# An instruction order from a timeline model: the scheduler of a hybrid-backbone kernel is given another machine model

## The chip, the cores and the metric

The kernel runs on one core of one Trainium2 chip. The metric is the device time of one execution in microseconds (us), the median of several runs. TensorE does the matmuls (PE; its weight loads are listed as PEld), VectorE is DVE, ScalarE is ACT, GpSimd is POOL, and SyncE (SP) issues most of the DMAs.

## The reference

One trunk layer over 256 latent and 256 context tokens of width 2048. One input projection feeds three mixers, which run in both directions over the tokens; each is projected, gated and merged, and a mixture of experts (MoE) follows.

```
u_lat = _modulate(_rmsnorm(x, g_norm1[i]), mod_lat[0], mod_lat[1])
cl = jnp.split(u_lat @ w_in, points, axis=-1)
ya_ctx, ya_lat = _bidirectional(_s5_direction, ...)      # A: S5, complex diagonal state
yb_ctx, yb_lat = _bidirectional(_rwkv_direction, ...)    # B: RWKV-7, matrix state, token by token
yc_ctx, yc_lat = _bidirectional(_gla_direction, ...)     # C: gated linear attention, chunks of 64
pa = _s5_out(ya, cols[0], s5_d, s5_w_glu)
pb = _rwkv_out(yb, cols[2], rw_g_up, rw_ln_w, rw_ln_b, rw_w_proj)
pc = _gla_out(yc, cols[7], gl_norm_g, gl_w_proj)
y = (gate_a * pa + gate_b * pb + gate_c * pc) @ w_out
x = x + mod_lat[2] * y_lat
v_lat = _modulate(_rmsnorm(x, g_norm2[i]), mod_lat[3], mod_lat[4])
x = x + mod_lat[5] * _moe(v_lat, ...)                    # top-1 group of 4, top-2 of its 8 experts
```

All operands are float32.

## The kernel before

**Dense work.** The large projections are done by `dense`. Each weight chunk is loaded by SP into `ww` (L348), rounded by ACT to `hw` (L350), and its remainder `lw` is formed by DVE, or at times by POOL (L355); the activations stand likewise as a rounded and a remainder tile (UH and UL; XA, XB, XC further on). Three matmuls, L386, L387 and L388, then add up hw·high, hw·low and lw·high; they are called dense matmuls below. A chunk is 12 of them. Buffers hold four `ww`, three `hw`, three `lw` and two accumulators `pd`.

**Stages, in time.** (1) The modulation vectors (weights `wm`, matmuls L256) and the input norm (L295, L297), while DVE prepares the S5 matrices (W of L1442 to L1448, used by the matmuls L1463). (2) S5 in two rounds, each for half of the states: the input matmuls L1552 fill a tile X; a scan of 63 steps on DVE (L1570 to L1573, four operations a step, each on the result of the one before) runs over X; then for four k and two directions DVE and POOL build an output matrix W (DVE L1594, L1596, L1598, L1599; POOL writes `wx` between), and matmuls L1615 and L1622 use it. There is one W buffer for each direction. (3) GLA. (4) RWKV-7 (L740 to L800): a chain of small matmuls and DVE steps from chunk to chunk; the second part of the modulation (L958, 64 loads of 1 MB into a single buffer `wm`) runs beside it. Its result `yo` leaves to DRAM by a DMA that POOL issues (L802). (5) `rw_out` loads it back as `yb` (L1173, on SP), takes each head's mean and variance (L1185 to L1197 on DVE, L1189 on ACT), transposes it (L62), multiplies it by the gate (L1206) and writes the operand XB. (6) Three branch projections: glu from XA, gl_proj from XC, rw_proj from XB; then w_out (L1226), the router (L1811) and the MoE, which streams 192 loads of 1 MB.

**What sets the order.** The source is written as Python generators that are merged in given proportions, so that dense work stands between the steps of the S5, GLA and RWKV chains. For instance,

```
merge((K.s5(), 320), (chainv(dense, n[0]), n[0]))
merge((chain(K.gla(sp), K.gla_out(sp)), 135), (chainv(dense, n[2]), n[2]))
K.rwkv(dense, steps, K.mods())
```

The order in which the source emits instructions is their priority. The framework's scheduler then goes through a model of the machine, takes for each engine a ready instruction of the best priority, and writes that order into the program. [...] Dense jobs of the S5 stage write through buffers of a pool that is closed when the stage ends, and those of the GLA stage through another, so dense work of a later stage cannot be taken in an earlier one.

## Time and profile before

| | us |
|---|---|
| median of 3 runs | 2418.14 (2417.78 to 2425.74) |
| the profiled execution | 2429.91 |
| its span in the trace | 2428.0 |
| PE busy | 2202.4 |
| DVE busy | 1451.3 |
| ACT busy | 922.8 |
| POOL busy | 440.3 |
| mean granted TensorE clock | 0.95 of full speed |

A busy time is the union of an engine's work. The span is 1.9 us shorter than the execution that it was taken from, which is itself 11.8 us above the median. In the page's slices PE is busy at eight to nine tenths or more until about 1800 us; after about 2000 us the DMA engines are full instead.

### The profile page before, as it was taken

To read this page: it belongs to the slowest core of one execution; us is meant where nothing else is said; L and a number is where in the kernel's file an instruction comes from. 1 tells how busy PE (TensorE), PEld (TensorE's weight loads), DVE (VectorE), ACT (ScalarE), POOL (GpSimd) and SP (SyncE) were. 2 spreads that over 40 slices of the span, in tenths; PEclk is the share of its full clock that TensorE was granted. 3 is DMA by queue.
4 is the path that set the end of the run, shared out by engine and by line. 5 is a ranking of instruction groups with operands and counts; after the bars stand their busy time and mean duration, and the time that the engine had idled before them with its cause. 6 is when DMAs were issued, how large, how long until landed. Compare 5 with 4: busy or idle time off the path is not lost. (4 is left out here: it accounts for less than half of the span.)

```text
span 2428.0 us, 49729 instructions
## 1 busy us (share of the span) xinstructions
PE 2202.4 (91%) x19317; PEld 1582.0 (65%) x19317; DVE 1451.3 (60%) x3816; ACT 922.8 (38%) x1833; POOL 440.3 (18%) x705
## 2 busy tenths in 40 slices
PE   7899989989989999999999999999998988887775
PEld 2447668767676777777888888988996753332211
DVE  8954967967666665656687877786764432211112
ACT  2235225236543434344445454543543431111111
POOL 2422033031212222222232222320021000000000
PEclk9999999989999999999999999999999989998876
DMA  7763332433276667667333232455667799999997
GB/s 287 289 213 105 126 112 85 131 121 107 88 254 212 229 216 246 227 208 236 101 116 99 94 115 90 127 161 163 201 200 261 241 380 422 421 421 421 421 422 297
DMA packets 188723, 526.05 MB, mean 217 GB/s; under 512 B 21376, under 2 KB 46992, under 8 KB 163520
## 3 DMA queue, kind: packets, MB, share of 16 engines
q1 hardware_dynamic: 172464, 500.14, 57.6%
q10 hardware_dynamic: 14160, 16.36, 1.9%
q0 software_dynamic: 1856, 6.29, 0.7%
q8 instruction: 154, 2.52, 0.4%
q14 instruction: 89, 0.73, 0.1%
HBM read 502.16 MB, written 19.51 MB: 215 GB/s over the span
## 5 line engine op out<-in xcount | busy, mean ns | idle before, releaser
L350 ACT CAST hw<-ww 128x512 fp32r<-128x512 f32 x556 | 340.2, 617 | 618.1 <-PE pd L387 505.3
L386 PE MATMUL pd<-UH,hw 128*128 128x256 f32 (+2 forms) x1648 | 566.0, 343 | 8.8 <-ACT hw L350 4.4
L388 PE MATMUL pd<-UH,lw 128*128 128x256 f32 (+2 forms) x1648 | 543.3, 330 | 10.1 <-DVE lw L355 7.0
L387 PE MATMUL pd<-UL,hw 128*128 128x256 f32 (+2 forms) x1648 | 538.8, 327 | 0.0
L355 DVE TENSOR_TENSOR lw<-ww,hw 128x512 fp32r<-128x512 f32 x544 | 389.6, 719 | 221.3 <-ACT hw L350 209.4
L386 PEld LDWEIGHTS pd<-UH,hw 128*128 128x128 f32 (+1 forms) x1648 | 314.3, 191 | 62.0 <-issue 14.1
L388 PEld LDWEIGHTS pd<-UH,lw 128*128 128x128 f32 (+1 forms) x1648 | 314.7, 191 | 57.7 <-DVE lw L355 13.6
L387 PEld LDWEIGHTS pd<-UL,hw 128*128 128x128 f32 (+1 forms) x1648 | 315.4, 191 | 37.0 <-issue 14.6
L1876 ACT ACTIVATE xg<-pm,modT,a 128x128 f32<-128x128 f32 x128 | 46.1, 484 | 307.2 <-PE pe L1900 283.9
L1900 PE MATMUL pe<-mw,xg 128*32 128x512 f32 x1024 | 139.1, 661 | 25.8 <-DMA mw<-in_moe_gu_dram 25.8
L1900 PEld LDWEIGHTS pe<-mw,xg 128*32 128x32 f32 x1024 | 27.7, 113 | 110.9 <-DMA mw<-in_moe_gu_dram 64.9
L1980 POOL TENSOR_TENSOR acc<-acc,mw 128x512 f32<-128x512 f32 x2 | 3.4, 1718 | 480.9 <-ACT acc L1979 480.9
L958 PE MATMUL pmod<-wm,sil 128*32 128x512 f32 x512 | 68.2, 605 | 21.6 <-DMA wm<-in_w_mod_dram 21.3
L1921 PE MATMUL pdn<-mw,ht 128*32 128x512 f32 x512 | 81.3, 697 | 3.5 <-ACT ht L1914 3.3
L1929 PE MATMUL pm<-ysl,owt 128*128 128x512 f32 x128 | 65.2, 633 | 20.4 <-DVE ysl L1926 20.4
L1873 PEld LDWEIGHTS pm<-oh,m 128*128 128x128 f32 x512 | 61.5, 197 | 25.5 <-issue 25.5
L388 PE MATMUL pd<-XAh,lw 128*128 128x256 f32 x256 | 73.3, 286 | 3.5 <-DVE lw L355 3.5
L256 PE MATMUL pmod<-wm,silu 128*32 128x512 f32 x256 | 62.3, 645 | 15.4 <-DMA wm<-in_w_mod_dram 14.7
L1909 DVE TENSOR_TENSOR hd<-hd,pe 128x256 f32<-128x256 f32 x8 | 3.4, 422 | 121.5 <-ACT hd L1908 121.5
L355 DVE TENSOR_TENSOR lx<-wx,hx 128x512 fp32r<-128x512 f32 x64 | 43.3, 691 | 53.8 <-ACT hx L350 52.9
L743 DVE TENSOR_TENSOR vz<-psa,z 32x256 f32<-32x256 f32 x120 | 50.1, 418 | 41.0 <-PE psa L740 39.2
L386 PE MATMUL pd<-XAh,hw 128*128 128x256 f32 x256 | 74.0, 289 | 0.0
(578 smaller groups left out, 4346.5 us busy)
## 6 DMA issues: line engine op xcount, KB each, us to landing
mw<-in_moe_gu_dram SPq DMA_DIRECT2D x128, 1024.0 KB, 19.8
wm<-in_w_mod_dram SPq DMA_DIRECT2D x64, 1024.0 KB, 5.4
mw<-in_moe_d_dram SPq DMA_DIRECT2D x64, 1024.0 KB, 19.7
ww<-in_w_gate_dram SPq DMA_DIRECT2D x192, 256.0 KB, 3.0
ww<-in_w_cols_dram SPq DMA_DIRECT2D x132, 256.0 KB, 2.9
wm<-in_w_mod_dram SPq DMA_DIRECT2D x64, 512.0 KB, 6.1
ww<-in_w_rkv_dram SPq DMA_DIRECT2D x96, 256.0 KB, 2.9
ww<-in_glu_dram SPq DMA_DIRECT2D x64, 256.0 KB, 2.9
```

Of the source, the lines that this page charges most:

```text
L256: nc.tensor.matmul(pt[32 * j:32 * j + 32, :], self.silu[:, k, :], w[:, k2, :], start=k < 4, stop=k >= 12, tile_position=(0, 32 * j))
L350: nc.scalar.copy(h, w)
L355: eng.tensor_tensor(l, w, h.bitcast(FT), op=OP.subtract)
L386: nc.tensor.matmul(ov, h[:, k2, :], uh, start=k == 0, stop=False)
L387: nc.tensor.matmul(ov, h[:, k2, :], ul, start=False, stop=False)
L388: nc.tensor.matmul(ov, l[:, k2, :], uh, start=False, stop=k == nk - 1)
L743: nc.vector.tensor_tensor(vz[bq, e, tt::2, :].rearrange(V, h=2), psa[bq, :, 0:128].rearrange("p h (d v) -> p h d v", d=2), z[bq, tt::2, :] ...
L958: nc.tensor.matmul(pt[32 * j:32 * j + 32], self.sil[:, 2 * kq + j, win], w[:, j], start=u == 0 and kq == 0, stop=u == 15 and kq == 6, tile ...
L1873: nc.tensor.matmul(p[:, 128 * (k % 4):128 * (k % 4) + 128], self.x2[:, t, 128 * k:128 * k + 128], oh[:, t, :], start=t == 0, stop=t == 1)
L1900: nc.tensor.matmul(pe[32 * e:32 * e + 32, :], xg[:, k, 32 * e:32 * e + 32], w[:, e, :], start=k == 0, stop=k == 15, tile_position=(0, 32 * e))
L1921: nc.tensor.matmul(py[32 * e:32 * e + 32, :], ht[:, f, 32 * e:32 * e + 32], w[:, e, :], start=f == 0, stop=f == 1, tile_position=(0, 32 * e))
L1929: nc.tensor.matmul(pr, owt[:, 128 * t:128 * t + 128], ys, start=True, stop=True)
```

## The change

A class of the name `tile` takes the place of the imported module. Its only function hands on the context with one more argument, so that the scheduler orders the instructions by its timeline model.

```
-import concourse.tile as tile
+import concourse.tile as _tile
...
+class tile:
+
+
+    @staticmethod
+    def TileContext(nc):
+        return _tile.TileContext(nc, schedule_with_timeline_sim=True)
+
```

Everything below moves down by 8 lines, so L386 is L394 in the changed kernel, and L1615 is L1623. The computing instructions, their engines, tiles and buffers are the same ones; their order on each engine is another. The rows below are the instruction lists of an engine, before and after; xN is a run of N alike, and the numbers behind the names tell tiles of one name apart.

**PE, the second round of S5**, at the last input matmuls (first piece) and at the first output matmuls (second piece) before the change. Between them stand 302 dense matmuls, and no other work.

```order
L388 MATMUL pd_4009<-UH_134,lw_4058 128x256
L386 MATMUL pd_4009<-UH_134,hw_4056 128x256
L1552 MATMUL pm_4153<-ug_1582,tr_4134 64x64 x14
L387 MATMUL pd_4009<-UL_135,hw_4056 128x256
L388 MATMUL pd_4009<-UH_134,lw_4058 128x256
```

```order
L1615 MATMUL py_5032<-W_5033,X_1581 32x128 x8
L1615 MATMUL py_5032<-W_5051,X_1581 32x128 x8
L386 MATMUL pd_5047<-UH_134,hw_4970 128x512
L387 MATMUL pd_5047<-UL_135,hw_4970 128x512
L388 MATMUL pd_5047<-UH_134,lw_4972 128x512
L1615 MATMUL py_5032<-W_5033,X_1581 32x128 x8
L1615 MATMUL py_5032<-W_5051,X_1581 32x128 x8
L386 MATMUL pd_5047<-UH_134,hw_5000 128x512
```

The same place after:

```order
L396 MATMUL pd_5635<-UH_134,lw_5664 128x256
L1560 MATMUL pm_4153<-ug_1582,tr_4134 64x64 x16
L1623 MATMUL py_5032<-W_5033,X_1581 32x128 x8
L1623 MATMUL py_5032<-W_5051,X_1581 32x128 x8
L1623 MATMUL py_5032<-W_5033,X_1581 32x128 x8
L1623 MATMUL py_5032<-W_5051,X_1581 32x128 x8
L1630 MATMUL py_5032<-T_5062,ug_1582 32x128 x8
L1623 MATMUL py_5032<-W_5129,X_1581 32x128 x8
L1623 MATMUL py_5032<-W_5140,X_1581 32x128 x8
```

The dense matmuls have moved ahead of the input matmuls; none is left between the last input matmul and the last output matmul of the round.

**DVE, the end of the same scan**, before and then after; L1573 (L1581 after) ends a step, and L355 forms an `lw`.

```order
L1573 TENSOR_TENSOR X<-X,s5t_5008 128x2x32
L355 TENSOR_TENSOR lw<-ww,hw 128x512
L1570 TENSOR_TENSOR s5t_5019<-LRI,X 128x64
L1571 TENSOR_TENSOR s5t_5020<-LRI,X 128x64
L1572 TENSOR_TENSOR X<-X,s5t_5019 128x64
L1573 TENSOR_TENSOR X<-X,s5t_5020 128x64
L355 TENSOR_TENSOR lw<-ww,hw 128x512 x2
L1594 TENSOR_TENSOR W<-s5KP,s5c 128x576
```

```order
L1581 TENSOR_TENSOR X<-X,s5t_5008 128x2x32
L1578 TENSOR_TENSOR s5t_5019<-LRI,X 128x64
L1579 TENSOR_TENSOR s5t_5020<-LRI,X 128x64
L1580 TENSOR_TENSOR X<-X,s5t_5019 128x64
L1581 TENSOR_TENSOR X<-X,s5t_5020 128x64
L1602 TENSOR_TENSOR W<-s5KP,s5c 128x576
L1604 TENSOR_TENSOR W<-s5KP,s5c 128x576
L1606 TENSOR_TENSOR W<-W,wx 128x576
```

The 26 L355 that stood within this scan are gone from it, and none stands among the builds of W that follow.

**PE, from the end of RWKV to `rw_out`**, before and then after. L798 (L806) is the last matmul of the chain, `yb` is the result loaded back.

```order
L388 MATMUL pd_21196<-XAh_19794,lw_21182 128x256
L798 MATMUL pj_20989<-z_20680,anti_5398 128x128 x2
L62 MATMUL pm_21003<-ident_82,modT_132 16x128
L386 MATMUL pd_21196<-XAh_19794,hw_21180 128x256
L387 MATMUL pd_21196<-XAl_19795,hw_21180 128x256
```

```order
L795 MATMUL py2_20922<-vz_20185,lmr_19984 32x64
L806 MATMUL pj_20989<-z_20680,anti_5398 128x128 x2
L70 MATMUL pm_21003<-ident_82,modT_132 16x128
L70 MATMUL pm_22081<-ident_82,yb_21017 128x128
L1214 MATMUL pm_22086<-glo_21022,gup_21020 128x256
L70 MATMUL pm_22152<-ident_82,yb_21017 128x128
```

Before, 513 rows of the glu projection (XA) stand between L62 on modT and the first L62 on yb; after, they stand earlier, between the steps of the RWKV chain, and the two L70 follow each other. In the RWKV stage the median number of dense matmuls between two L740 (L748) is 24 before and 39 after.

## Rows read from the trace of the kernel before

**Rows 1.** The page: busy us, share of the span and instructions of each engine.
```profile
PE 2202.4 (91%) x19317; PEld 1582.0 (65%) x19317; DVE 1451.3 (60%) x3816; ACT 922.8 (38%) x1833; POOL 440.3 (18%) x705
```

**Rows 2.** Windows: start:end, length, busy us of each engine (instructions), PEclk, DMA, GB/s.
```profile
407.00:516.00 109.00, 100.24 (x728) 78.37 (x723) 90.23 (x312) 27.51 (x51) 21.19 (x15) 0.95 0.37 113
...
700.00:1670.00 970.00, 941.88 (x10786) 767.03 (x10785) 685.57 (x1994) 450.35 (x880) 244.98 (x518) 0.99 0.51 166
1670.00:1780.00 110.00, 106.47 (x952) 105.52 (x951) 80.58 (x156) 58.58 (x109) 0.69 (x1) 0.98 0.63 196
1780.00:1965.00 185.00, 159.82 (x843) 133.28 (x841) 95.16 (x199) 71.94 (x140) 23.25 (x28) 0.91 0.75 257
1965.00:2428.00 463.00, 355.76 (x2224) 133.34 (x2224) 86.61 (x163) 65.61 (x177) 3.40 (x2) 0.85 0.97 402
```

**Rows 3.** Timeline of DVE, scan of round two: start, us, engine, line; one undisturbed step.
```profile
431.17 0.23 DVE L1570 TENSOR_TENSOR s5t<-LRI,X 128x64 f32<-128x64 f32 x1
...
431.96 0.23 DVE L1570 TENSOR_TENSOR s5t<-LRI,X 128x64 f32<-128x64 f32 x1
```

**Rows 4.** Windows over that scan and over the outputs behind it.
```profile
420.00:476.00 56.00, 53.34 (x248) 42.49 (x247) 52.39 (x249) 16.45 (x31) 0.00 (x0) 1.00 0.44 135
476.00:514.00 38.00, 32.43 (x408) 24.52 (x407) 26.34 (x29) 4.61 (x8) 16.53 (x11) 0.87 0.32 94
```

**Rows 5.** Timeline of DVE, six builds of W behind that scan: first and last row.
```profile
479.11 0.75 DVE L1594 TENSOR_TENSOR W<-s5KP,s5c 128x576 f32<-128x576 f32 x1
...
507.71 0.74 DVE L1599 SCALAR_TENSOR_TENSOR W<-W,wx 128x576 f32<-128x576 f32 x1
```

**Rows 6.** Groups of one line from 476 to 514 us: count, busy, mean ns, idle before.
```profile
L1615 PE MATMUL py<-W,X 64*32 64x128 f32 x256 | 10.5, 314 | 5.6 <-DVE W L1598 5.6
L1622 PE MATMUL py<-T,ug 128*32 128x128 f32 x64 | 2.6, 279 | 0.0
```

**Rows 7.** Windows around the router: PE before and behind a pause.
```profile
1960.00:1970.00 10.00, 6.02 (x27) 5.92 (x28) 5.65 (x38) 0.20 (x1) 0.00 (x0) 0.50 1.01 424
1970.00:1980.00 10.00, 10.00 (x87) 4.60 (x85) 0.00 (x0) 3.01 (x8) 0.00 (x0) 0.97 0.72 279
```

**Rows 8.** Timeline row, then line views, in `rw_out`: count, ns min/median/max, first and last start.
```profile
1675.28 0.69 POOL L802 DMA_DIRECT2D dyb<-yo  x1 [6.14 <-DVE yo L800]
...
DMA to landing us min/median/max: 2.5/2.6/4.0
...
L1173 SPq DMA_DIRECT2D yb<-dyb x2: 327/370/412, 1678.1 to 1678.9; - x2
...
DMA to landing us min/median/max: 5.6/6.0/6.5
...
L1185 DVE TENSOR_REDUCE rws<-yb x4: 676/678/686, 1683.7 to 1688.4; 128x8 f32<-128x512 f32 x4
...
L1197 DVE TENSOR_TENSOR yb<-yb,rws x4: 684/684/692, 1701.7 to 1707.6; 128x512 f32<-128x512 f32 x4
...
L62 PE MATMUL pm<-ident,yb x16: 270/272/273, 1740.7 to 1775.3; 128*128 128x128 f32 x16
```

**Rows 9.** Line views of the input norm on DVE.
```profile
L295 DVE RECIPROCAL fo<-fo x1: 3339/3339/3339, 59.3 to 59.3; 128x512 f32<-128x512 f32 x1
...
L297 DVE TENSOR_TENSOR xT<-xT,fo x16: 684/685/692, 62.7 to 71.7; 128x512 f32<-128x512 f32 x16
```

**Rows 10.** Timeline of PE in RWKV: dense matmuls behind a chain step; start, us.
```profile
1200.01 0.38 PE L386 MATMUL pd<-UH,hw 128*128 128x256 f32 x1
1200.23 0.28 PE L387 MATMUL pd<-UL,hw 128*128 128x256 f32 x1
1200.35 0.28 PE L388 MATMUL pd<-UH,lw 128*128 128x256 f32 x1
```

**Rows 11.** Waits of PE: us in total, times, longest.
```profile
PE pmod L958 <- DMA wm<-in_w_mod_dram: 21.3, 21, 2.5
...
PE py L1615 <- DVE W L1598: 10.8, 6, 2.5
```

## The prediction

> **What bounds the kernel now.** The first view is the page's busy times: PE works for 2202 of 2428 us [rows 1], so the kernel is close to PE-bound, and what counts is when PE stands still. The windows say where. From 700 to 1670 us PE idles for 28 of 970 us, from 1670 to 1780 for 3.5 of 110, from 1780 to 1965 for 25 of 185, and in the second S5 round (407 to 516) for 9 of 109 [rows 2]. From 1965 us the MoE stream holds the DMA engines at a share of 0.97 and 402 GB/s [rows 2]; that stage is bound by its bytes, which the change leaves alone, so whatever is lost or won before the router moves the end by as much. I therefore work out PE's idle time before 1965 us, at each place where the new order changes what PE has to do while it waits for another engine. One fact makes the sum simple: the PE instructions are the same ones, so dense work that is moved is not lost; it stands earlier, and the cost of a move is the idle time where cover is taken away less the idle time where it is put.

> **1. The second S5 round.** The scan is a chain on DVE: a step takes 431.96 - 431.17 = 0.79 us when nothing stands between [rows 3], so 63 steps take 50 us at least. Before, 302 dense matmuls lay beside it, and PE idled for 56.0 - 53.3 = 2.7 us in the scan and for 38.0 - 32.4 = 5.6 us in the outputs behind it [rows 4]. After, PE has nothing at all between the last input matmul and the first output matmul, nor between the four groups of outputs. It must stand through the scan, and then through the builds of W. Six of the eight builds took from 479.1 to 508.5 us, 4.9 us each, with some L355 among them [rows 5]; four undisturbed operations of 0.75 us make 3.0 us [rows 5]. Eight builds thus take 24 to 39 us; I take 31, near the middle, as the L355 are gone but the POOL products that share the work are not. In that time PE does its own 10.5 + 2.6 = 13.1 us [rows 6]. PE's idle time becomes 50 + 31 - 13 = 68 us, against 8 before: +60. [...] Term: **+63**, from 53 (builds at 24) to 74 (builds at 39, clock 6). Its cover was the dense work that is now done earlier, in the first round and between the input matmuls, where PE had little idle time to give back. DVE is 26 L355 lighter in this scan, which shortens the scan but does not spare PE the wait.

> Whether PE could fill that pause from further down its list is decided by the same place in the trace: it waited 10.8 us in six pieces for W at L1615 [rows 11], though dense matmuls stood right behind. [...]

> **2. The turn from RWKV to `rw_out`.** Before, the glu projection covered it: from 1670 to 1780 us PE was busy for 106.5 of 110 us [rows 2]. After, all of glu and gl_proj is between the chain steps, and behind the chain's last matmul PE has only the transposes of `yb`. What it waits for: about 1 us to `yo`, the issue on POOL, 0.7, its landing, 2.6, and the load on SP, 6.0 [rows 8]; then the head statistics. From the first L1185 to the end of the last L1197 they took 1708.3 - 1683.7 = 24.6 us with much L355 between, and their own work is twelve DVE operations, 8.2 us (four each of L1185 and L1197 of 0.68 us [rows 8], and four of L1188, which are of their size), with ACT's squares between, some 2.5 us by the same size. So 20.5 to 35 us to the transposes; then about 2 us to the first XB operand, and the clock's 3. With less L355 between I take 24 + 2 + 3 = **+29**, from 22 to 40. [...]

> **3. The start.** DVE now does the input norm ahead of the first W: 3.3 + 16 x 0.685 = 14.3 us [rows 9], which the matmuls L1463 wait for behind it. At the same time the norm's users come earlier. Between 0 and 14; **+7**.

> **4. The load waits in RWKV.** The single `wm` buffer costs PE 21.3 us in 21 waits [rows 11]. They come where two groups of L958 stand close together: counted in PE's lists, before, 20 of the 63 gaps hold fewer than 21 dense matmuls, after 9 do. Waits in that proportion leave 9.6 us: **-12**, from -21 to 0.

> **5. Fewer changes between dense and small matmuls.** The dense matmul behind a chain step holds PE for 0.22 us against 0.12 for the next ones [rows 10]. There are 1129 changes between dense and other work before and 723 after, so 203 fewer such starts: up to 203 x 0.10 = 20 us. Small matmuls that now stand longer in one run may pay for themselves, so **-10**, from -20 to 0.

> **6. The rest.** Half of the W waits [rows 11] are of the first S5 round, which now has more dense work beside it: -3. GLA and the router I cannot tell apart from before: 0, from -10 to 10. The MoE stream and its loads: 0.

> Sum: 63 + 29 + 7 - 12 - 10 - 3 = **+74 us**; all terms at their low ends +19, at their high ends +140. The profiled execution, 2429.9 us (span 2428.0 and 1.9 around it), would become 2504. It lay 11.8 us over the median of the runs, so on the median the forecast is 2418 + 74 = **2492 us**.

> **The rivals.**

> (a) *Only one pause shows.* If RWKV's chain ends well ahead of the last dense matmul that stands among it, `yo` is stored and loaded under cover, or the statistics, with no L355 between, take no longer than their 11 us and the start costs nothing: +74 - 29 - 7 = +38, 2456 us. [...]

> (b) *Faster: the dense work that is moved closes idle time elsewhere.* Place: RWKV and the branches. Price: all of the wm waits (21), all of the starts (20), the W waits of round one (5) and PE's idle time from 1780 to 1965 (25) [rows 2], together -71. For that to win, the two pauses must cost less than 71 together; halved S5 idle (30) and rw_out at 22 give 52 - 71 = -19, 2399 us. Against it: nothing in the trace halves 63 dependent steps, and the idle time from 1780 belongs to w_out and the router, which have no dense work to be moved to.

> (c) *No difference*: gains as in (b) against both pauses at their low ends, 75 - 71 = +4, 2422 us. The same evidence speaks against it.

> (d) *Much slower: the RWKV chain becomes the bound.* The median gap between two L740 holds 39 dense matmuls now, 24 before, while the dense work is the same; if its stock is used up at places, PE would wait for the chain there as in the S5 scan. If 100 of the chain's us lost their cover by half, +50 more: 2542 us. For it: the model behind the new order seems to think the S5 scan shorter than it is, and might misjudge this chain alike. Against it: dense work stands between the chain's steps up to its end.

> That the order is not changed at all is excluded: PE's list alone reads otherwise from its first rows on.

> **How the numbers follow.** The forecast, both pauses, 2460 to 2530 us: 0.58. (a) 0.14, (b) 0.08, (c) 0.08, (d) 0.12. Range 2418 to 2545: it leaves out (b), half of (c) and a third of (d), some 0.16. A difference of 0.5%, 12 us, is about what a measurement of this kernel can tell. Faster by more: (b), 0.08. Within: (c) with a part of (a), 0.09. Slower: 0.83.

> **What would show each step.** In the changed kernel's trace: PE without work for some 50 us between the last L1560 and the first L1623 of round two, DVE with scan steps of 0.79 us and no L363 among them; waits of L1623 for W of some 15 us behind; a pause of 20 to 35 us between L806 and L70 on yb, with half clock behind each; waits of L966 for wm near 10 us; the MoE stage as long as before. Wrong would be: dense matmuls in progress while the scan runs; a rw_out pause under 15 us; waits on `vz`, `S` or `psa` in RWKV that add up to tens of us.

## The result, and the profile after

The changed kernel takes 2552.4 us (median of four runs, 2546.2 to 2562.2) against 2418.0 us before, a ratio of 1.0535 (95% interval 1.0499 to 1.0571): 134 us slower. The direction was forecast, the size was not: 2492 was predicted, and 2552 lies above the range's end of 2545. The profiled execution took 2552.94 us with a span of 2551.2 us; that is 123 us more than the profiled execution of before, which itself lay 12 us over its median.

The page of the changed kernel, with its busy times (against [rows 1]) and the slices of PE and of its granted clock:

```profile
PE 2193.1 (86%) x19317; PEld 1596.6 (63%) x19317; DVE 1457.1 (57%) x3816; ACT 915.0 (36%) x1831; POOL 447.1 (18%) x705
...
PE   4999999449959999998999898999958979877775
...
PEclk8899999759979999998989898999969979888887
```

PE does not work longer, 2193 against 2202 us; it stands still longer, 358 against 226 us. Slices of 63.8 us with a 4 or 5 stand at the start (the first), in the second S5 round (the eighth and ninth), in GLA (the twelfth) and at the turn to `rw_out` (the thirtieth). The slices between look nearly full, but many of them are at a clock of 8 or 9 tenths.

Where the time went is read from windows cut at the same events in both traces: the last L1463, the last L1622, the first L740 on S, the last L798, the first L1226, the first L1900, the end (in the changed kernel the same lines plus 8). Columns as in [rows 2]. Before:

```profile
0.00:146.00 146.00, 123.81 (x922) 51.33 (x924) 124.29 (x309) 38.77 (x73) 50.93 (x51) 0.96 0.77 279
146.00:514.30 368.30, 344.57 (x2609) 259.26 (x2608) 260.59 (x741) 130.78 (x261) 82.87 (x67) 0.96 0.38 118
514.30:794.80 280.50, 254.86 (x1800) 196.54 (x1800) 182.91 (x455) 148.49 (x276) 52.76 (x75) 0.95 0.50 166
794.80:1674.20 879.40, 861.28 (x10094) 706.71 (x10094) 623.23 (x1799) 410.26 (x801) 226.38 (x481) 1.00 0.49 160
1674.20:1833.40 159.20, 149.65 (x1183) 147.20 (x1182) 109.53 (x212) 78.75 (x151) 16.84 (x18) 0.96 0.66 206
1833.40:1971.00 137.60, 117.11 (x517) 92.17 (x516) 66.74 (x153) 50.94 (x99) 7.09 (x11) 0.90 0.78 277
1971.00:2428.00 457.00, 351.09 (x2203) 128.76 (x2202) 84.03 (x148) 64.79 (x175) 3.40 (x2) 0.86 0.97 402
```

After:

```profile
0.00:159.70 159.70, 122.25 (x940) 55.79 (x944) 122.29 (x311) 39.21 (x75) 46.41 (x51) 0.88 0.74 272
159.70:563.40 403.70, 331.37 (x2640) 261.50 (x2639) 271.71 (x753) 130.83 (x265) 86.05 (x72) 0.89 0.34 105
563.40:850.90 287.50, 244.01 (x1736) 188.03 (x1732) 174.76 (x441) 143.48 (x268) 51.11 (x70) 0.92 0.43 139
850.90:1876.20 1025.30, 971.78 (x10878) 818.58 (x10877) 688.87 (x1916) 451.24 (x883) 236.48 (x482) 0.95 0.49 160
1876.20:1953.70 77.50, 55.34 (x419) 52.16 (x418) 48.62 (x98) 35.47 (x69) 17.28 (x18) 0.86 0.54 174
1953.70:2095.90 142.20, 118.74 (x543) 96.75 (x542) 66.91 (x155) 51.92 (x103) 6.42 (x11) 0.88 0.75 270
2095.90:2551.20 455.30, 349.64 (x2177) 123.74 (x2176) 83.90 (x148) 62.83 (x170) 3.39 (x2) 0.85 0.97 404
```

The lengths can't be compared directly, since dense matmuls have moved from one stage to another. Counted in PE's lists, RWKV now holds 757 more of those with 256 columns (3520 against 2763) and 16 more L966 (70.8 us for 256 of them, so 0.28 each). A dense matmul behind another takes 0.12 us [rows 10]; with 0.117 (three such steps from 1899.13 to 1899.48 us in the changed kernel) the two make 93 us (the median step in both traces is 0.119, which would move the two rows with most moved work by some 2 us); S5 holds 48 more, GLA 40 fewer, the turn 765 fewer. With that taken off:

| stage | before | after | moved work | same work | idle of PE | forecast |
|---|---|---|---|---|---|---|
| start | 146.0 | 159.7 | 0 | +14 | +15 | +7 |
| S5 | 368.3 | 403.7 | +6 | +30 | +49 | +60 |
| GLA | 280.5 | 287.5 | -9 | +16 | +18 | 0 |
| RWKV | 879.4 | 1025.3 | +93 | +53 | +35 | -22 |
| turn and w_out | 296.8 | 219.7 | -90 | +12 | +16 | +29 |
| MoE | 457.0 | 455.3 | 0 | -2 | 0 | 0 |

The largest single miss is RWKV: 53 us lost where 22 were to be won. PE's waits in the changed kernel (us in total, times, longest), to be set against [rows 11]:

```profile
PE py L1623 <- DVE X L1581: 54.7, 1, 54.7
...
PE pm L1471 <- DVE W L1455: 21.4, 2, 19.1
PE pm L70 <- DVE yb L1205: 18.1, 1, 18.1
PE pm L70 <- DVE gla L1070: 17.4, 2, 14.0
PE pu L764 <- DVE vz L751: 13.2, 21, 1.2
...
PE py L1623 <- DVE W L1606: 10.1, 6, 2.4
PE pmod L966 <- DMA wm<-in_w_mod_dram: 9.9, 8, 2.5
```

The two pauses of the forecast are there, the one of S5 as a single wait of 54.7 us. The new kind is in the line of L764: 21 short waits of PE for one chain step on DVE. Before, L756 has no such wait.

Such a place in RWKV, from the timeline of PE (start, us; in brackets the idle time before and what ended it); no dense matmul stands between these three:

```profile
1313.41 0.46 PE L764 MATMUL pu<-vz,kb 64*64 64x64 f32 x8 [0.63 <-DVE vz L751]
1314.31 0.42 PE L748 MATMUL psa<-S,wl 64*32 64x64 f32 x8 [0.45 <-DVE S L780]
1315.27 0.70 PE L764 MATMUL pu<-vz,kb 64*64 64x64 f32 x8 [0.53 <-DVE vz L751]
```

And the windows around it, 5 us each:

```profile
1305.00:1310.00 5.00, 5.00 (x30) 3.59 (x28) 1.10 (x2) 1.75 (x4) 0.00 (x0) 1.00 0.30 96
1310.00:1315.00 5.00, 3.65 (x49) 3.05 (x48) 1.82 (x5) 2.08 (x6) 2.93 (x8) 0.97 0.18 64
1315.00:1320.00 5.00, 3.98 (x32) 3.21 (x32) 1.83 (x5) 2.42 (x6) 2.35 (x9) 0.50 0.00 0
1320.00:1325.00 5.00, 2.44 (x16) 2.19 (x17) 4.18 (x10) 2.33 (x4) 1.44 (x4) 0.50 0.00 2
1325.00:1330.00 5.00, 4.53 (x37) 3.56 (x38) 3.38 (x7) 1.20 (x2) 2.07 (x4) 0.50 0.00 0
```

PE is fully busy until 1310, then waits about half a microsecond at many of the steps, and from 1315 the granted clock is 0.50, although PE still works for about half of the time or more. Over the whole stage the clock's mean is 0.95 where it was 1.00, and PE's busy time for the same work is 971.8 - 93 - 861.3 = 17 us longer. So the 53 us of RWKV are 35 us of idle time and 17 us of busy time.

This is not spread over the stage. In PE's list of the changed kernel five stretches without any dense matmul hold 9 to 13 groups of chain matmuls (L748, L764) each; before, no such stretch holds more than two. In the trace they are these:

```profile
1170.30:1198.90 28.60, 21.80 (x326) 13.30 (x325) 13.94 (x31) 9.54 (x20) 10.36 (x27) 0.76 0.45 160
1310.00:1328.50 18.50, 13.10 (x128) 10.49 (x127) 10.86 (x23) 8.03 (x17) 7.41 (x23) 0.63 0.05 18
1424.90:1447.60 22.70, 16.40 (x164) 13.20 (x162) 12.72 (x28) 10.70 (x21) 8.76 (x26) 0.70 0.06 19
1545.10:1568.60 23.50, 17.81 (x180) 14.06 (x178) 12.95 (x29) 10.69 (x21) 9.69 (x27) 0.68 0.06 18
1855.10:1876.60 21.50, 13.32 (x238) 9.97 (x237) 7.12 (x21) 0.97 (x2) 2.41 (x6) 0.55 0.07 21
```

They are 115 of the 1025 us, and 32 of the stage's 53.5 us of idle time lie in them; what is left, 21 us, is near the 18 us of the whole stage before. The granted clock is 0.55 to 0.76 in them and 0.98 or 0.99 between them. That the half clock is what makes the 17 us of busy time fits this, but no run shows it by itself.

### The profile page after: what moved, and what is told of

It reads as the page before. It is cut to its first block, busy times and chain, and to the rows that moved or that the text cites. A ratio compares the mean times of both kernels' runs of the same rounds, so it can differ in the third digit from the quotient of the medians.

```text
span 2551.2 us, 49730 instructions
## 1 busy us (share of the span) xinstructions
PE 2193.1 (86%) x19317; PEld 1596.6 (63%) x19317; DVE 1457.1 (57%) x3816; ACT 915.0 (36%) x1831; POOL 447.1 (18%) x705
## 3 DMA queue, kind: packets, MB, share of 16 engines
q1 hardware_dynamic: 172464, 500.14, 54.7%
## 5 line engine op out<-in xcount | busy, mean ns | idle before, releaser
L394 PE MATMUL pd<-UH,hw 128*128 128x256 f32 (+2 forms) x1648 | 541.1, 328 | 13.3 <-ACT fo L925 6.5
L363 DVE TENSOR_TENSOR lw<-ww,hw 128x512 fp32r<-128x512 f32 x544 | 394.4, 727 | 245.4 <-ACT hw L358 233.3
L394 PEld LDWEIGHTS pd<-UH,hw 128*128 128x128 f32 (+1 forms) x1648 | 314.1, 191 | 54.1 <-issue 9.5
L1908 PE MATMUL pe<-mw,xg 128*32 128x512 f32 x1024 | 147.4, 684 | 40.9 <-DMA mw<-in_moe_gu_dram 40.7
L1623 PE MATMUL py<-W,X 64*32 64x128 f32 x512 | 23.2, 355 | 68.7 <-DVE X L1581 54.7
L966 PE MATMUL pmod<-wm,sil 128*32 128x512 f32 x512 | 70.8, 621 | 10.0 <-DMA wm<-in_w_mod_dram 9.9
L363 DVE TENSOR_TENSOR lx<-wx,hx 128x512 fp32r<-128x512 f32 x64 | 43.6, 694 | 55.5 <-ACT hx L358 55.3
L394 PE MATMUL pd<-XAh,hw 128*128 128x256 f32 x256 | 73.4, 287 | 0.0
L395 PE MATMUL pd<-XAl,hw 128*128 128x256 f32 x256 | 73.2, 286 | 0.0
```

Source lines behind the costliest of these rows:

```text
L363: eng.tensor_tensor(l, w, h.bitcast(FT), op=OP.subtract)
L394: nc.tensor.matmul(ov, h[:, k2, :], uh, start=k == 0, stop=False)
L395: nc.tensor.matmul(ov, h[:, k2, :], ul, start=False, stop=False)
L966: nc.tensor.matmul(pt[32 * j:32 * j + 32], self.sil[:, 2 * kq + j, win], w[:, j], start=u == 0 and kq == 0, stop=u == 15 and kq == 6, tile ...
L1623: nc.tensor.matmul(py[g2][32 * c:32 * c + 32, ks], X[gs, q0:q0 + 32, 16 * r + 4 * k + c], W[d][gs, r, c, w0:w0 + 128], start=d == 0 and r ...
L1908: nc.tensor.matmul(pe[32 * e:32 * e + 32, :], xg[:, k, 32 * e:32 * e + 32], w[:, e, :], start=k == 0, stop=k == 15, tile_position=(0, 32 * e))
```

## The experiments

All times are medians of four runs or more, beside runs of the kernel before on the same chip; the ratio is to these, with its 95% interval. Three ways of changing an order are used: an order of issue between two instructions of one engine (no wait), an engine's list given as a whole in that way, and a merge weight of the source.

### Dense work held at its place, stage by stage

The first four are the changed kernel with dense matmuls put behind a chain matmul that the source emits before them. The helpers:

```
+    def mm(self, *a, **k):
+        self.last = self.nc.tensor.matmul(*a, **k).ins.name
+
+    def hold(self, m):
+        if self.pin and self.last:
+            self.tc.add_manual_dep(m.ins, self.last, mybir.DependencyInfo(
+                mybir.DependencyClass.NoSync, mybir.DependencyReason.DATA), reason="order")
...
-                nc.tensor.matmul(ov, h[:, k2, :], uh, start=k == 0, stop=False)
+                self.hold(nc.tensor.matmul(ov, h[:, k2, :], uh, start=k == 0, stop=False))
```

with `self.mm` in place of `nc.tensor.matmul` in the chain, and `pin` set to True for the stage.

**The second S5 round.** In `s5`, ahead of the scan:

```
+            self.pin = rd == 1
             LR, LI = LRI[:, 0, rd], LRI[:, 1, rd]
```

> The changed kernel (timeline order) with one addition: in the second S5 round every dense matmul is put, in PE's list, behind the S5 matmul that the source emits before it. PE's list then has 306 dense matmuls between the last input matmul and the first output matmul (changed kernel: 0; before: 302), and 135 among the output matmuls; the rest of the list stays nearly as in the changed kernel. Theory (the time is lost where PE's list leaves it nothing to do while another engine works): the 54.7 us wait for X and most of the 14 us of waits for W go, some 49 to 57 us in all (the stage's idle time grew by 49), so 2552 becomes 2495 to 2503. Rival 1 (the dense work is missed elsewhere as soon as it stands here, so the wait only moves): 2530 to 2552. Rival 2 (dense work with its DVE parts lengthens the scan from 50 to 70 us, so only part comes back): 2515 to 2525.

Measured: 2535.8 us, ratio 1.0471 (1.0437 to 1.0504), some 16 us less than the changed kernel. The pause is closed, the wait for X falls from 54.7 to 8.2 us. But windows of the first round, where its outputs are made, and of the second scan show what it cost:

```profile
360.00:370.00 10.00, 5.07 (x84) 2.88 (x80) 7.46 (x9) 0.00 (x0) 4.59 (x4) 0.50 0.24 55
370.00:380.00 10.00, 5.06 (x84) 2.84 (x80) 7.47 (x9) 0.00 (x0) 4.59 (x4) 0.50 0.04 5
...
450.00:460.00 10.00, 10.00 (x44) 8.04 (x43) 9.36 (x44) 2.29 (x4) 0.00 (x0) 1.00 0.45 144
```

The same two windows of the first round in the changed kernel:

```profile
360.00:370.00 10.00, 10.00 (x113) 7.61 (x112) 8.41 (x11) 1.53 (x3) 5.82 (x4) 1.00 0.51 133
370.00:380.00 10.00, 10.00 (x108) 7.40 (x110) 8.16 (x12) 2.63 (x5) 4.58 (x4) 1.00 0.53 136
```

The dense work that fills the second scan is now missing beside the first round's outputs, where PE is busy for half of the time, at half clock. The stage has a fixed stock of it; filling one hole opened another. Over the stage PE's idle time falls from 72 to 40 us, but its busy time rises from 331 to 353 us for the same matmuls. Rival 1 holds for most of it.

**The turn to `rw_out`.** `pin` is True around `merge((K.rw_out(...), XB), 25), (dense, 300))`, with the chain's matmuls as `mm`.

> The changed kernel with one addition: the dense matmuls that the source emits beside rw_out are put behind the last matmul of the RWKV chain. 170 of them then stand between it and the first transpose of yb (changed kernel: 0; before: 513). Theory: the 18 us wait for yb goes, and with it the half clock behind; 170 matmuls of 0.117 us are 20 us of cover: 2552 becomes 2530 to 2540. If the term of the prediction (29 us) was right and only hidden in the ledger: 2523. Rival (the work taken away from the RWKV chain opens as much idle time there as it closes here, since that chain now has 127 instead of 105 links without dense work between): 2545 to 2560.

Measured: 2575.0 us, ratio 1.0622 (1.0592 to 1.0652), slower still. PE's idle time in the turn falls from 22 to 5 us, as expected, but in RWKV, from which the work was taken, it rises from 53 to 77 us and the clock falls from 0.95 to 0.92. The work held back is missing between the chain's steps: PE's waits for `vz` are 34.2 us where they were 21.6, and the one for `z` ahead of L806 (here in the helper's line) goes from 1.4 us to 5.3 in two pieces. The rival holds, and more than that.

**RWKV and `rw_out`.** `pin` is True from RWKV's beginning.

> The changed kernel with every dense matmul of the RWKV stage and of rw_out put behind the RWKV chain matmul that the source emits before it. Of the links of the chain (an L748 or L764 group and what follows) 19 of 173 then have no dense matmul behind them (changed kernel: 105 of 201; before: 5 of 151), and rw_out has its 170. Theory (RWKV lost 35 us of PE time because chain steps stand next to each other and each exposes the half microsecond of its DVE step): the stage's idle time falls from 53 to about 20 us and the yb wait goes: 2552 becomes 2500 to 2510. Rival (RWKV's waits come from DVE's own order, where the chain's additions stand behind the lw operations, and not from PE's): idle time stays near 50, time 2530 to 2540 as in the run that pins rw_out alone.

Measured: 2543.6 us, ratio 1.0482 (1.0443 to 1.0521). The turn is closed (5 us idle), but RWKV still idles for 62 us in 934, at a clock of 0.95: close to the rival's numbers. Its reason does not hold, though: PE's waits for the chain's additions `vz` are down to some 4 us. Dense work stands between the chain's steps again (of the five stretches without it only the last is left), and PE waits for other things, for `wm` and for what the chain's preparation makes (L354 is the helper's line; L589, L542 and L975 are L572, L525 and L958 of before):

```profile
PE pmod L975 <- DMA wm<-in_w_mod_dram: 21.4, 14, 3.5
...
PE pm L70 <- ACT nb L542: 10.1, 8, 1.9
PE psa L354 <- DVE lmk L589: 8.5, 6, 3.6
```

So the theory that the place of the dense matmuls alone was the cause of RWKV's loss fell here.

**All stages.** `pin` is True from S5 to `rw_out`, with GLA's matmuls as `mm` too.

> The changed kernel with the dense matmuls of S5, GLA, RWKV and rw_out all put behind the chain matmul that the source emits before them; PE's interleaving is then close to before's (scan one 309 dense matmuls, scan two 309, rw_out 158, 20 of 174 links without dense work), while DVE, ACT, POOL and SP keep an order that the timeline model chooses. Theory (PE's order is the cause of all but the start): the idle time of S5 (49), GLA (18), RWKV (35) and rw_out (13) comes back, 2552 becomes 2430 to 2445; the start (15 us later at the last L1471) stays. Rival (the other engines' orders carry a good part of it): 2470 to 2510.

Measured: 2555.4 us, ratio 1.0545 (1.0514 to 1.0575): no gain at all over the changed kernel, although each hole that the forecast named has its dense work again. The expectation was 2430 to 2445. The trace shows new waits in the place of the old: GLA takes 325 us where it took 287.5 (some 10 us of this are dense matmuls that now stand there), with waits for `gla` of 38.5 us in four pieces, and RWKV idles for 63 us, as in the run before. What had to be explained was no longer where the dense work stands, but the rest of the lists.

### Whole lists

The other kernels take the list of an engine from one kernel and leave the rest to the scheduler of the other. The lists stand in the file as compressed numbers of the instructions, which are the same in both:

```
+    traced = {i.name: i for i in block.bb.instructions}
+    for text in LISTS.values():
+        steps = np.frombuffer(zlib.decompress(base64.b85decode(text)), np.int32)
+        names = [n for n in ("I-%d" % v for v in np.cumsum(steps)) if n in traced]
+        for a, b in zip(names, names[1:]):
+            tc.add_manual_dep(traced[b], a, mybir.DependencyInfo(
+                mybir.DependencyClass.NoSync, mybir.DependencyReason.DATA), reason="order")
```

**All five lists from before**, under the timeline scheduler, as a control:

> A control for the given lists: the timeline scheduler with the lists of all five engines taken from before. What is left to the scheduler are buffers, semaphores and table loads. If lists are all that matters: 2415 to 2430, the same as before. If giving a list costs something by itself, or the buffers that the scheduler hands out matter: slower, and the runs with given lists have to be read with that cost taken off.

Measured: ratio 1.000 (0.9968 to 1.0032). The lists are all there is to this change; buffers, semaphores and the giving of a list cost nothing that shows.

**PE's list from before:**

> The timeline scheduler, but PE's list is given: that of the kernel before, instruction by instruction. The other engines' lists follow from the scheduler with that constraint and come near to before's too (counted in pairs that stand the other way round than in before: DVE 11,932, where the changed kernel has 87,740; SP 5,812 against 9,738). Theory A (PE's list carries the loss; pinning the dense work alone did not bring it back because the small matmuls of RWKV's preparation stayed where the timeline model put them): 2420 to 2445. Theory B (what is left in the other engines' lists, DVE's and SP's, carries it): 2500 to 2560.

Measured: 2494.3 us, ratio 1.0292 (1.0248 to 1.0336): 2.4 of the 5.35 percent come back, some 58 us. 70 us are lost with PE's list unchanged. By stages: start, S5 and RWKV.

```profile
0.00:160.90 160.90, 127.69 (x922) 53.69 (x924) 125.20 (x309) 38.25 (x73) 47.91 (x51) 0.90 0.72 258
160.90:546.80 385.90, 349.33 (x2610) 264.15 (x2609) 262.13 (x742) 132.48 (x263) 78.96 (x67) 0.93 0.37 111
...
829.10:1734.90 905.80, 872.59 (x10095) 711.51 (x10094) 636.73 (x1799) 408.99 (x801) 233.28 (x481) 0.99 0.49 156
```

Against the windows of before that is 15, 18 and 26 us, with the same PE instructions in the same order. PE waits longer for other engines and for loads, in S5 for instance 17.0 us for X.

**DVE's list from before:**

> The timeline scheduler with DVE's list of the kernel before; PE's list then differs from before's in 104,945 pairs (changed kernel: 1,677,385). Theory A (PE's list): since PE's list comes near to before's by itself, most returns, but not all: 2430 to 2480. Theory B in the form that DVE's list is the cause: 2420 to 2440. If neither PE's nor DVE's list matters but SP's or ACT's: 2500 to 2560.

Measured: 2514.8 us, ratio 1.0356 (1.0309 to 1.0403). PE's list, free, does not fit it: 56.6 us of waits for `lw`, 46 times.

**The lists of the changed kernel under the usual scheduler**, PE's and DVE's:

> The usual scheduler, as in the kernel before, but PE's list is given: that of the changed kernel. DVE then differs from the changed kernel's list in 14,542 pairs only, SP in 7,327. Theory A (PE's list carries the loss, through the two pauses, the exposed chain steps and the half clock behind them): 2535 to 2560. Theory B (the other engines' lists carry a good part): 2440 to 2500.

> The usual scheduler with DVE's list of the changed kernel; PE's list comes near to the changed kernel's (153,062 pairs the other way round). Theory A and the form of B with DVE: 2530 to 2560. If SP or ACT is the cause: 2420 to 2450.

Measured: 2622.8 us, ratio 1.0806 (1.0778 to 1.0835), and 2657.8 us, ratio 1.0941 (1.0907 to 1.0976). Both are slower than the changed kernel itself, beyond every expectation. A list of the changed kernel, with the others made around it by the usual scheduler, is worse than either whole; a list of before under the timeline scheduler (2494 and 2515 us above) lies between the two.

**Which engine carries the 70 us.** PE's list together with SP's, with DVE's, with ACT's and POOL's, and with all three of these:

> The timeline scheduler with the lists of PE and SP from before; DVE, ACT and POOL are free (DVE then stands 7,032 pairs from before's list). The run with PE's list alone took 2494 us. If SP's order of loads is what was left (21 loads of wm in a row ahead of the first ww at the start, wm later in RWKV): 2420 to 2440. If DVE, ACT and POOL carry it: 2480 to 2500.

> The timeline scheduler with the lists of PE, DVE, ACT and POOL from before; SP alone is free. The counterpart of the run with PE and SP: if SP's order is what was left, 2480 to 2500; if DVE, ACT and POOL carry it, 2420 to 2440.

> The timeline scheduler with the lists of PE and DVE from before; ACT, POOL and SP are free. PE's list alone gave 2494, PE with DVE, ACT and POOL 2440. If DVE's list carries what was left (chain steps behind lw operations, the norm ahead of the first W): 2440 to 2455. If ACT's or POOL's: 2475 to 2495.

> The counterpart: the lists of PE, ACT and POOL from before, DVE and SP free. If DVE's list carries what was left: 2480 to 2495. If ACT's (its casts hw feed every dense matmul, and its copies stand in the chains) or POOL's: 2440 to 2455.

| lists from before, under the timeline scheduler | ratio | 95% interval |
|---|---|---|
| none (the changed kernel) | 1.0535 | 1.0499 to 1.0571 |
| PE | 1.0292 | 1.0248 to 1.0336 |
| PE, SP | 1.0264 | 1.0238 to 1.0290 |
| PE, ACT, POOL | 1.0306 | 1.0274 to 1.0338 |
| PE, DVE | 1.0154 | 1.0101 to 1.0207 |
| PE, DVE, ACT, POOL | 1.0039 | 1.0020 to 1.0058 |
| all five | 1.0000 | 0.9968 to 1.0032 |

SP's list adds nothing clear of the intervals to PE's. ACT's and POOL's add nothing without DVE's, and 1.15 points with it (half a point of which is within the interval of the run with PE and DVE). DVE's adds 1.4 points to PE's. PE's list alone brings 2.4 points, DVE's alone 1.8, both 3.8: nearly the sum. In the other direction nothing adds up: PE's list of the changed kernel costs 8.1 percent under the usual scheduler, where all of the changed kernel costs 5.4.

**Cut by stage.** Lists of all five engines from before, for what the source emits up to the end of S5, and for what it emits from RWKV on:

> The changed kernel, with the lists of all five engines from before for everything that the source emits up to the end of S5; GLA and all behind it stay as the timeline model orders them. By the stages of the two traces, start and S5 together end 49 us later than before, of which 6 us are dense matmuls done earlier: 2552 becomes 2500 to 2515. If the stages are not independent (what is won there is lost behind): 2530 to 2552.

> The counterpart: the lists of all five engines from before for everything emitted from RWKV's beginning on; start, S5 and GLA stay as the timeline model orders them. From the first chain step of RWKV to the first expert matmul the changed kernel takes 1245 us, before 1176, with the same work: +69. 2552 becomes 2475 to 2490. If the prediction's terms for this part were right (rw_out +29, waits for wm -12, fewer changes -10, together +7): 2540 to 2550.

Measured: 2508.8 us, ratio 1.0347 (1.0315 to 1.0379), 44 us less than the changed kernel, as expected. And 2504.7 us, ratio 1.0327 (1.0293 to 1.0362), 48 us less where 62 to 77 were expected. GLA and RWKV in this second one:

```profile
561.20:874.50 313.30, 253.62 (x1756) 190.27 (x1752) 177.02 (x445) 144.74 (x270) 50.98 (x71) 0.88 0.44 142
874.50:1751.00 876.50, 859.35 (x10094) 705.24 (x10094) 623.37 (x1799) 410.16 (x801) 227.69 (x481) 1.00 0.49 161
```

From RWKV's first chain step to the first expert matmul it takes 1173 us against 1245 in the changed kernel, 72 less, at a clock of 1.00 in RWKV and 17 us of idle time there: the whole of the expectation. The difference is in GLA, which is 26 us longer than in the changed kernel (313.3 against 287.5): there PE's waits for `gla` are 26.0 us instead of 17.4, and one wait for `wm` takes 10.1 us. If the gains of the two runs add up, about 1.4 percent are left, 33 us. GLA is the only stage whose order neither run gives back; it is 33 us longer than before in the second and 13 us in the first, so that the whole rest lies in it is not shown.

### The S5 pause alone, in the kernel before

The usual scheduler, and one number:

```
-                merge((K.s5(), 320), (chainv(dense, n[0]), n[0]))
+                merge((K.s5(), 176), (chainv(dense, n[0]), n[0]))
```

> The kernel before, with its usual scheduler, and one number changed: the weight of the S5 stage against its dense work is 176 instead of 320, so that the dense work is used up before the second scan (no dense matmuls between its last input and its first output matmul, and none among the outputs; before: 302 and 70). It does the first part of the change alone. By the prediction's term: +50 to +63, 2470 to 2485. By the run that put dense work back into the second scan of the changed kernel and won only 17 us: +15 to +30, 2435 to 2450.

Measured: 2486.6 us, ratio 1.0249 (1.0207 to 1.0291): 60 us. The wait for X is 53.7 us, and the S5 stage takes 433.3 us with 83 us of idle time and a clock of 0.89 (47 dense matmuls more than before stand in it, some 6 us):

```profile
146.50:579.80 433.30, 350.05 (x2656) 267.95 (x2656) 274.05 (x754) 134.56 (x267) 87.63 (x72) 0.89 0.34 104
```

Taken by itself, the first term of the prediction (+63, from 53 to 74) is right.

## Why the prediction was right or wrong

**The sign, and the views that gave it: right.** The MoE stage is 2 us shorter, so everything ahead of the router went to the end, as argued. PE's busy time is the same within 9 us, since it grew by 17 us in RWKV and fell by 19 in S5; the loss is idle time, 358 us against 226.

**1. The second S5 round, +63: right as an isolated term, too large in the sum.** PE waits 54.7 us for X and 14.1 us for W (10.1 for L1606 and 4.0 for L1607), 68.8 us, where 68 were worked out; the experiment that does this part alone costs 60 us. But the S5 stage as a whole lost 30 us. The forecast let the dense work moved ahead of the scan win back nothing ("where PE had little idle time to give back") but 3 us for the first round's waits. It won back 12 us of idle time elsewhere in the stage (23.7 - 8.2 = 15.5 before, 72.3 - 68.8 = 3.5 after), and PE's busy time for the same work is some 19 us shorter (331.4 - 5.6 against 344.6). Changes between dense and other matmuls fall there from 213 to 90; at the prediction's 0.10 us for each start that is 6 us, and where the rest comes from is open. PE took nothing past the one wait of 54.7 us (0.00 us of work in each window of 10 us from 480 to 530); that shows little of what it could take, since nothing but the round's outputs stood behind that wait in this stage. The trace of before shows more: L386 of a dense job starts at 484.10 us, PE then idles 1.29 us until the L1615 of 485.89 has its W, and L387 on the same `hw` follows only at 486.30. No run shows the 3 us that terms 1 and 2 put on the clock behind a pause. What the trace after shows, beside [rows 7], is a granted clock of 0.50 in every window of 10 us from 480 to 570 us, through the pause and the outputs behind it; and behind the wait of 18.1 us at the turn 0.50 until 1898 us and 1.00 from 1901 to 1906.

**2. The turn to `rw_out`, +29: the mechanism right, the term too large.** The pause is there, as one wait of 18.1 us, less than the lower end of 20.5 (its parts add up to 21.0). The whole chain of store, load and statistics lies in it. The statistics took 13.4 us, from 1883.0 to 1896.4, between the 10.7 and the 24.6 of the prediction; but the first load of `yb` landed 3.3 us after its issue instead of 6.0, and the transposes started behind the first of the four L1205 instead of the last.

```profile
1882.98 1.28 DVE L1193 TENSOR_REDUCE rws<-yb 128x8 f32<-128x512 f32 x2 [6.17 <-DMA yb<-dyb]
...
1893.88 2.50 DVE L1205 TENSOR_TENSOR yb<-yb,rws 128x512 f32<-128x512 f32 x4
```

Turn and w_out together lost 12 us. Nor can it be won back alone: closing it by taking dense work out of RWKV cost more there than it brought.

**3. The start, +7 from 0 to 14: mis-sized.** It cost 14 us, the upper end. PE waits 19.1 us in one piece for a W that stands behind the norm in DVE's list. That the norm's place alone does it is not shown: with PE's list of before, and also with DVE's, the start still ended at 161 us. With both it ended at 152, with ACT's and POOL's besides at 149, against 146 before.

**4. The waits for wm, -12: right.** PE's waits went from 21.3 [rows 11] to 9.9 us, where 9.6 were worked out.

**5. Fewer changes between dense and small matmuls, -10: the step that failed.** The count was right, 1129 against 723, but only one side of it was priced: where a change disappears in a chain, dense work that stood behind a chain step is gone from there. Of the pairs of successive groups of L748 and L764 in PE's list, 58 of 246 have no dense matmul between them in the changed kernel, and 3 of 239 before (the expectations above count links in another way, 105 of 201 against 5 of 151). The prediction looked at the median of the gaps that hold some (24 and 39) and not at those that hold nothing. 52 of the 58 empty pairs stand in the five stretches shown above, where PE idles for 32 us and the clock falls. RWKV lost 35 us of idle time and 17 us of busy time, where terms 4 and 5 promised a gain of 22.

This is what rival (d) described, PE waiting for the RWKV chain at places without dense work. It was given 0.12, and the range left out a third of it. The argument against it, that dense work stands between the chain's steps up to its end, is what the list contradicts: the last of the five stretches is the chain's end. It was not for want of stock, since dense work follows the other four. One of the prediction's own signs of being wrong came up, too: waits for `vz`, `S` and `sh` in RWKV add up to 28 us. That the total came out near (d)'s 2542 us is partly luck, since S5 lost 30 us less than its term while GLA and the start lost more than theirs. That RWKV's loss is a matter of order is shown by the run with the lists of before from RWKV on (idle 17 us, clock 1.00). That the empty pairs are its only cause is not: with dense work put back between them, RWKV idled as long, for `wm` and the products of its preparation.

**6. The rest, 0 for GLA: wrong by omission.** GLA lost 16 us for the same work: PE waits 17.4 us for `gla` in two pieces, a third pause of the kind of the two that were found. The lists show it: 50 dense matmuls stand right ahead of the last of the four groups of L62 on `gla` before, and none in the changed kernel, where PE waits 14.0 us there. (The high ends of the terms add up to 138 us, not 140; nothing hangs on it.)

**A step that was not there at all:** the sum treated the change as one of PE's list, with the other engines' lists as fixed durations around it. With PE's list of before, 70 us remain, and nearly all of it goes only when DVE's and then ACT's and POOL's lists come back too. Counted in this sequence, the lists of DVE, ACT and POOL are worth 2.9 - 0.4 = 2.5 of the 5.35 percent, some 61 us; in another sequence the shares would be others, as DVE's list alone brings 1.8 points and after PE's 1.4. Why ACT's and POOL's lists matter only beside DVE's is open; no run separates their single moves.

## What to carry to other kernels

When an order changes, count for every chain the links that have nothing beside them, not the median of what stands between, and do it on each chain of the program; short waits in a row can cost more than the one long pause that strikes the eye (53 us in RWKV, 30 in S5). A stock of filler work is finite: a hole that is filled is another that opens, so price a move by the whole stage. And engines that hand work to each other at every step are scheduled as a set: one engine's list of the changed kernel, put into the kernel before, was slower here than either whole.
